# Spatial products of 32 sample tokens: operands of 128 partitions with zeros instead of 32 partitions

## The chip, the cores and the metric

The kernel runs on one core of a Trainium2 chip. The metric is the device time of one execution in microseconds (us); three runs of the kernel before gave a median of 2195.8. The core has TensorE (PE, whose weight loads the profile lists as PEld), VectorE (DVE), ScalarE (ACT), GpSimd (POOL) and SyncE (SP), and 16 DMA engines. In this kernel nearly all DMAs are issued from SP's queue, in order.

## What is computed

The reference is one inference step of a two-layer encoder for two groups of tokens that share the weights: 1024 prompt tokens and 32 sample tokens, of 1024 channels. Layer 0 mixes tokens with a spatial gate, layer 1 with pooling; each layer ends with a channel MLP of 4096. The change touches the spatial gate alone:

```python
def sgu_mixer(h, w_in, g_v, w_s, b_s, w_out, T):
    z = jax.nn.gelu(h @ w_in)
    u, v = jnp.split(z, 2, axis=-1)
    v = rmsnorm(v, g_v)
    vr = v.reshape(bsz, L // T, T, SGU_GROUPS, SGU_GROUP_DIM)
    w = w_s[:, :T, :T] * sgu_chunk_mask()[:T, :T].astype(w_s.dtype)
    s = jnp.einsum('gij,bnjgd->bnigd', w, vr)
    s = s + jnp.transpose(b_s[:, :T])[None, None, :, :, None]
    s = s.reshape(bsz, L, D_SGU)
    return (u * s) @ w_out, v
```

T is 128 for the prompt (8 chunks) and 32 for the sample (one chunk of 32 tokens). There are 8 groups of 256 channels. So each group has, besides the prompt's products that sum over 128 tokens, one product that sums over the 32 sample tokens.

## The kernel before

**Tiling.** Channels lie on the partitions and tokens on the columns. `TILES` (L27) cuts the tokens into three tiles: 384 and 384 prompt tokens, and 256 prompt tokens with the 32 sample tokens behind them (`npr` = 256, `nsm` = 32, `nch` = 2 chunks). Only the third tile has sample tokens. The large products are done in split precision: `products` (L910 to L917) issues three matmuls for each term, high by high (L915), high by low (L916) and low by high (L917). Helpers record all VectorE operations under L79.

**The gating stage.** The v half of the input product is computed first, with tokens on the partitions, and stored in DRAM as `vd`, one row for each token, the sample's 32 rows last. `mixes` (L357) then lists the passes over pairs of groups and tiles, and `sgu_item` (L1208) does two groups of one tile:

- `up` (L1241) computes the u half, matmuls into `pu` at L915 to L917, and an activation (L1251). Before its first product it calls `inputs`, and after it `factors`.
- `inputs` (L1217) takes a buffer `vl` of 128 partitions x 3 x 256 and loads the chunks of the group from `vd` (L1219), and in the third tile the 32 sample rows into partitions 0 to 31 of the last slice (L1224). `vl` comes from a ring of three buffers (`x3`), which other small tiles share.
- `factors` (L1228) multiplies the transposed and masked spatial weights `wt` by the reciprocal norms `rv` of the tokens: one 128x128 block for each chunk (L1235), and a 32x32 block for the sample (L1237).
- `gate` (L1254) does the spatial products for two halves k of the group: for each chunk one fp32 product over 128 partitions (L1263), and in the third tile one over 32 partitions and 32 columns (L1271), into the same PSUM bank `psp`. VectorE then applies gain and bias and multiplies by u.
- `down` (L1303) is the product with `w_out`, into `po`; it runs later, among the `up` of the next item.

Each fp32 product shows as two weight loads and two matmuls in the profile. A gate thus has 12 passes: 2 x 3 chunks x 2 in the first two tiles, and 2 x (2 chunks + 1 sample) x 2 in the third. There are 24 gates, 8 of them in the third tile.

**Order.** Outside the first stage, which is written out by hand, a scheduler orders the instructions on each engine, with the estimated times that `tick` and `weave` keep to place the weight stream among the products. Weights come by DMA into three `raw` buffers, ScalarE writes the high part (L423), VectorE the low part (L79), into a ring of 16 buffers that TensorE frees. GpSimd has work in the first microseconds (the identity, small loads) and two additions at the end (L1651).

Of the kernel before, what the change touches and what calls it, by code (L numbers as in the profile page):

```python
# [12 lines left out]
ALU = mybir.AluOpType  # L13
AX = mybir.AxisListType

P = 128
# [18 lines left out]
def tile_stream_encoder_step(  # L35
# [25 lines left out]
    nc = tc.nc  # L61
# [11 lines left out]
    def on_dve(op, fixed, rate):  # L73
        def run(out, *args, **kw):
            n = 1
            for k in out.shape[1:]:
                n *= k
            time["dve"] += fixed + n / rate
            return op(out, *args, **kw)  # L79

        return run
# [3 lines left out]
    ts = on_dve(nc.vector.tensor_scalar, 0.1, 930.0)  # L85
# [48 lines left out]
    def ps_up(name):  # L134
        return psum.tile([P, 512], F32, tag="pu", bufs=2, name=name)
# [7 lines left out]
    def t_m(name):  # L143
        return work.tile([P, 384], F32, tag="m", bufs=3, name=name)
# [7 lines left out]
    def t_x(name, shape):  # L152
        return work.tile(shape, F32, tag="x3", bufs=3, name=name)
# [756 lines left out]
    def products(ps, n, terms):  # L910

        last = len(terms) - 1
        tick(3 * len(terms) * (0.004 + n / 2265.0))
        for i, (wh, wl, rh, rl) in enumerate(terms):
            mm(ps[:, :n], wh, rh, start=i == 0, stop=False)  # L915
            mm(ps[:, :n], wh, rl, start=False, stop=False)  # L916
            mm(ps[:, :n], wl, rh, start=False, stop=i == last)  # L917
# [191 lines left out]
    rv = const.tile([P, 9], F32, name="rv")  # L1109
# [98 lines left out]
    def sgu_item(p, t, mix, after):  # L1208
        gs, tiles = mixes[p]
        last = t == tiles[-1]  # L1210
        n = ncol[t]
        col0, npr, nsm = TILES[t]
        nch = npr // P
        hid = []
        vls, wrs = {}, {}

        def inputs(g):  # L1217
            vl = vls[g] = t_x(f"vl{g}_{t}", [P, 3, 256])
            nc.sync.dma_start(  # L1219
                vl[:, :nch, :],  # L1220
                vd[col0 : col0 + npr, g * 256 : (g + 1) * 256].rearrange("(c p) d -> p c d", p=P),
            )
            if nsm:
                nc.sync.dma_start(  # L1224
                    vl[:nsm, nch, :], vd[SEQ : SEQ + nsm, g * 256 : (g + 1) * 256]
                )

        def factors(g):  # L1228
            wt, _, turn = mix[g]
            while turn:  # L1230
                turn.pop()()
            wr = wrs[g] = t_m(f"wr{g}_{t}")
            for c in range(nch):
                b = col0 // P + c
                ts(wr[:, c * P : (c + 1) * P], wt, rv[:, b : b + 1], None, op0=ALU.mult)  # L1235
            if nsm:
                ts(wr[:nsm, npr : npr + nsm], wt[:nsm, :nsm], rv[:nsm, 8:9], None, op0=ALU.mult)  # L1237

        us = []

        def up(g, k):  # L1241
            if k == 0:
                inputs(g)
            ps = ps_up(f"pu{g}_{t}_{k}")
            products(ps, n, up_terms(("u", p, g, k), t))
            if k == 0:
                factors(g)
            if last:
                w_finish(("u", p, g, k))
            u = t_m(f"u{g}_{t}_{k}")  # L1250
            act(out=u[:, :n], in_=ps[:, :n], func=AF.Gelu_apprx_tanh)  # L1251
            us.append(u)

        def gate(g):  # L1254

            vl, wr, bb = vls[g], wrs[g], mix[g][1]
            sps = []
            tick(0.48 * nch + 0.2)
            for k in range(2):
                sp = ps_dn(f"psp{g}_{t}_{k}")  # L1260
                sps.append(sp)
                for c in range(nch):
                    mm(  # L1263
                        sp[:, c * P : (c + 1) * P],
                        vl[:, c, k * P : (k + 1) * P],
                        wr[:, c * P : (c + 1) * P],
                        start=True,
                        stop=True,
                    )
                if nsm:  # L1270
                    mm(  # L1271
                        sp[:, npr : npr + nsm],
                        vl[:nsm, nch, k * P : (k + 1) * P],
                        wr[:nsm, npr : npr + nsm],
                        start=True,
                        stop=True,
                    )
            for k, sp in enumerate(sps):
                f = 2 * g + k
                s = t_c(f"s{g}_{t}_{k}")  # L1280
                stt(
                    out=s[:, :npr].rearrange("p (c j) -> p c j", j=P),
                    in0=sp[:, :npr].rearrange("p (c j) -> p c j", j=P),
                    scalar=gvT[:, f : f + 1],
                    in1=bb.unsqueeze(1).broadcast_to([P, nch, P]),
                    op0=ALU.mult,
                    op1=ALU.add,
                )
                if nsm:
                    stt(  # L1290
                        out=s[:, npr : npr + nsm],
                        in0=sp[:, npr : npr + nsm],
                        scalar=gvT[:, f : f + 1],
                        in1=bb[:, :nsm],
                        op0=ALU.mult,
                        op1=ALU.add,
                    )
                tt(out=s[:, :n], in0=s[:, :n], in1=us.pop(0)[:, :n], op=ALU.mult)
                a, b = t_hid("h", f"ush{g}_{t}_{k}"), t_hid("l", f"usl{g}_{t}_{k}")
                split(a, b, s, n)  # L1300
                hid.append((a, b))

        def down():  # L1303
            for d in range(KB):
                ps = ps_dn(f"po{gs[0]}_{t}_{d}")
                terms = []
                for j, (a, b) in enumerate(hid):
                    wh, wl = need_w(("o", p, gs[j // 2], d // 4))
                    o = (j % 2) * 512 + (d % 4) * P
                    terms.append((wh[:, o : o + P], wl[:, o : o + P], a[:, :n], b[:, :n]))  # L1310
                products(ps, n, terms)
                accumulate(t, d, ps, gs[0] == 0)
                if d == 0 and after is not None:
                    st = Stat(t, f"rs_{t}")
                if after is not None:
                    st.square(d)
                if last and d % 4 == 3:
                    for g in gs:
                        w_finish(("o", p, g, d // 4))
                weave(d % 2)  # L1320
            if after is not None:
                after(st)

        for j in range(4):
            up(gs[j // 2], j % 2)
            if j % 2 == 1:
                gate(gs[j // 2])
            weave()
            if j == 0:
                flush()  # L1330
        pending.append(down)
# [390 lines left out]
```

## Time and profile before

| | before |
|---|---|
| runs, median of 3 (lowest to highest) | 2195.8 us (2195.24 to 2196.72) |
| the profiled execution | 2196.44 us |
| its span, first to last instruction | 2194.7 us |
| mean granted TensorE clock | 0.998 |
| TensorE / VectorE / ScalarE / GpSimd busy | 99% / 63% / 45% / under 1% |
| the gating stage, first to last spatial product | 244.5 to 635.3 us |

How to read the lines of the profile. A timeline row gives start and duration in us, engine and line, operation, written<-read tiles by their names in the program, shapes and a count of merged instructions. For a matmul, "128*128 128x384" is the part of the array in use (partitions * columns of the stationary operand) and the moving operand. A row of a group gives the count, busy time and mean duration in ns, then the idle time of its engine just before and what ended it. A row of waits gives who waited for whom, the total in us, how many times and the longest. The ends of matmuls are modelled, so that two of them overlap in the record; starts are what to compare.

### The profile page before, as it was taken

The numbers are of one execution on the slowest core, as the hardware profiler recorded it, in microseconds if no ns is written. First come the engines' busy times: TensorE is split into PE (matmuls) and PEld (weight loads), VectorE is DVE, ScalarE is ACT, GpSimd is POOL, SyncE is SP. The second block draws the span as 40 slices with busy tenths as digits, with TensorE's granted clock in tenths as the row PEclk, the third lists the DMA queues.
The fourth block names the chain that finished last, engine by engine and source line by source line (L and its number), as shares of the span: only waits on it lengthen the run. The fifth ranks groups of instructions, "written<-read, shape, count | busy, mean of one in ns | idle before, by whom it ended". The sixth has DMA issues, their size and how long they took to land.

```text
span 2194.7 us, 33441 instructions
## 1 busy us (share of the span) xinstructions
PE 2177.2 (99%) x13383; PEld 2095.6 (95%) x13383; DVE 1374.9 (63%) x2431; ACT 987.9 (45%) x1683; POOL 5.4 (0%) x12
## 2 busy tenths in 40 slices
PE   8999999999999999999999999999999999999998
PEld 5777999999999999999999999999999999999998
DVE  6756656466769546575647779869675553523375
ACT  5533422234447552323445566666564542313355
POOL 0000000000000000000000000000000000000000
PEclk9999999999999999999999999999999999999999
DMA  8475633353437443344545466565454542302342
GB/s 292 163 240 166 193 97 121 91 156 104 138 101 233 130 150 120 106 133 123 179 128 163 139 189 186 161 196 156 143 171 135 162 154 60 106 10 77 99 123 108
DMA packets 354865, 312.99 MB, mean 143 GB/s; under 512 B 10834, under 2 KB 316538, under 8 KB 354708
## 3 DMA queue, kind: packets, MB, share of 16 engines
q1 hardware_dynamic: 354452, 310.61, 45.7%
q8 instruction: 105, 1.72, 0.3%
q14 instruction: 52, 0.43, 0.1%
q10 hardware_dynamic: 128, 0.14, 0.0%
q0 software_dynamic: 128, 0.09, 0.0%
HBM read 278.95 MB, written 31.84 MB: 142 GB/s over the span
## 4 chain that ended last, share of the span: by engine, by line
PE 98%; ACT 1%; DMA 0%; DVE 0%; issue 0%; POOL 0%; POOLq 0%; SPq 0%; ACTq 0%; DVEq 0%
PE pf L915 12%; PE pf L917 11%; PE pg L915 11%; PE pg L917 11%; PE pg L916 11%; PE pf L916 11%; PE pu L915 3%; PE pu L917 3%; PE po L915 3%; PE po L916 3%; PE po L917 3%; PE pu L916 3%; PE pv L942 2%; PE pv L943 2%; PE pv L944 2%; PE psp L1263 1%
## 5 line engine op out<-in xcount | busy, mean ns | idle before, releaser
L915 PE MATMUL pf<-hh,wh_up 128*128 128x384 f32 (+1 forms) x1536 | 502.6, 327 | 0.0
L915 PE MATMUL pg<-fh,wh_dn 128*128 128x384 f32 (+1 forms) x1536 | 498.0, 324 | 0.0
L917 PE MATMUL pf<-hh,wl_up 128*128 128x384 f32 (+1 forms) x1536 | 496.5, 323 | 0.0
L917 PE MATMUL pg<-fh,wl_dn 128*128 128x384 f32 (+1 forms) x1536 | 494.8, 322 | 0.0
L916 PE MATMUL pg<-fl,wh_dn 128*128 128x384 f32 (+1 forms) x1536 | 494.6, 322 | 0.0
L916 PE MATMUL pf<-hl,wh_up 128*128 128x384 f32 (+1 forms) x1536 | 490.5, 319 | 0.0
L915 PEld LDWEIGHTS pg<-fh,wh_dn 128*128 128x128 f32 x1536 | 288.8, 188 | 4.4 <-issue 3.3
L79 DVE TENSOR_TENSOR wl_up<-raw,wh_up 128x1024 fp32r<-128x1024 f32 x152 | 185.9, 1224 | 167.3 <-ACT wh_up L423 167.3
L915 PEld LDWEIGHTS pf<-hh,wh_up 128*128 128x128 f32 x1536 | 288.2, 188 | 1.3 <-issue 0.8
L916 PEld LDWEIGHTS pg<-fl,wh_dn 128*128 128x128 f32 x1536 | 288.6, 188 | 0.7
L916 PEld LDWEIGHTS pf<-hl,wh_up 128*128 128x128 f32 x1536 | 288.6, 188 | 0.4
L917 PEld LDWEIGHTS pg<-fh,wl_dn 128*128 128x128 f32 x1536 | 288.5, 188 | 0.0
L917 PEld LDWEIGHTS pf<-hh,wl_up 128*128 128x128 f32 x1536 | 288.0, 187 | 0.0
L423 ACT ACTIVATE wh_up<-raw 128x1024 fp32r<-128x1024 f32 x152 | 161.1, 1060 | 276.8 <-PE pf L916 214.3
L79 DVE TENSOR_TENSOR acc<-acc,pg 128x384 f32<-128x384 f32 (+1 forms) x336 | 174.0, 518 | 166.5 <-PE pg L917 165.3
L423 ACT ACTIVATE wh_dn<-raw 128x1024 fp32r<-128x1024 f32 x152 | 160.9, 1059 | 218.0 <-PE pg L916 180.9
L79 DVE TENSOR_TENSOR wl_dn<-raw,wh_dn 128x1024 fp32r<-128x1024 f32 x152 | 185.9, 1223 | 85.8 <-ACT wh_dn L423 85.6
L79 DVE SCALAR_TENSOR_TENSOR aa<-raw,csil,aa 128x512 f32<-128x512 f32 (+1 forms) x364 | 204.2, 622 | 2.0 <-DMA raw<-in_w_ada_dram 1.7
L1345 ACT ACTIVATE r<-pf 128x384 f32<-128x384 f32 (+1 forms) x192 | 86.5, 451 | 197.7 <-PE pf L917 197.5
L79 DVE TENSOR_TENSOR fl<-r,fh 128x384 fp32r<-128x384 f32 (+1 forms) x192 | 100.3, 522 | 104.3 <-ACT fh L1171 103.0
L915 PE MATMUL pu<-hh,wh_u 128*128 128x384 f32 (+1 forms) x384 | 127.9, 333 | 0.0
L915 PE MATMUL po<-ush,wh_o 128*128 128x384 f32 (+1 forms) x384 | 124.4, 324 | 0.0
(271 smaller groups left out, 2903.2 us busy)
## 6 DMA issues: line engine op xcount, KB each, us to landing
raw<-in_ffn_w_up_dram SPq DMA_DIRECT2D x152, 512.0 KB, 4.0
raw<-in_ffn_w_down_dram SPq DMA_DIRECT2D x152, 512.0 KB, 3.4
raw<-in_w_ada_dram SPq DMA_DIRECT2D x96, 512.0 KB, 4.1
raw<-in_sgu_w_in_dram SPq DMA_DIRECT2D x40, 512.0 KB, 4.4
xd<-acc SPq DMA_DIRECT2D x8, 1536.0 KB, 7.2
raw<-in_sgu_w_out_dram SPq DMA_DIRECT2D x24, 512.0 KB, 3.8
xo_r<-xd SPq DMA_DIRECT2D x32, 384.0 KB, 3.6
vd<-vt SPq DMA_DIRECT2D x32, 256.0 KB, 3.3
```

What stands on the lines that cost most here:

```text
L79: return op(out, *args, **kw)
L423: act(out=wh, in_=r, func=AF.Copy)
L915: mm(ps[:, :n], wh, rh, start=i == 0, stop=False)
L916: mm(ps[:, :n], wh, rl, start=False, stop=False)
L917: mm(ps[:, :n], wl, rh, start=False, stop=i == last)
L942: mm(ps[:m, :], a_h, wh[:, o : o + 512], start=k == 0, stop=False)
L943: mm(ps[:m, :], a_h, wl[:, o : o + 512], start=False, stop=False)
L944: mm(ps[:m, :], a_l, wh[:, o : o + 512], start=False, stop=k == KB - 1)
L1263: mm(sp[:, c * P : (c + 1) * P], vl[:, c, k * P : (k + 1) * P], wr[:, c * P : (c + 1) * P], start=True, stop=True,)
L1345: act(out=r[:, :n], in_=ps[:, :n], func=AF.Relu)
```

## The change

The rows of `vl` beyond the 32 sample rows are set to zero by GpSimd ahead of the small DMA, in the third tile only. The factor block of the sample becomes 128x32, with all 128 rows of `wt` and of `rv`, and both operands of the sample's product become 128 partitions high. The sum over partitions 32 to 127 adds zeros.

```diff
@@ inputs
             if nsm:
+
+                nc.gpsimd.memset(vl[:, nch, :], 0.0)
                 nc.sync.dma_start(
                     vl[:nsm, nch, :], vd[SEQ : SEQ + nsm, g * 256 : (g + 1) * 256]
                 )
@@ factors
             if nsm:
-                ts(wr[:nsm, npr : npr + nsm], wt[:nsm, :nsm], rv[:nsm, 8:9], None, op0=ALU.mult)
+                ts(wr[:, npr : npr + nsm], wt[:, :nsm], rv[:, 8:9], None, op0=ALU.mult)
@@ gate
                 if nsm:
                     mm(
                         sp[:, npr : npr + nsm],
-                        vl[:nsm, nch, k * P : (k + 1) * P],
-                        wr[:nsm, npr : npr + nsm],
+                        vl[:, nch, k * P : (k + 1) * P],
+                        wr[:, npr : npr + nsm],
                         start=True,
                         stop=True,
                     )
```

The built program has the same instructions in the same order on TensorE, VectorE, ScalarE and SP; GpSimd has eight more, the memsets of 128x256, in the order of the eight gates. Each small DMA into `vl` waits for its memset, and the first sample product of each gate waits for the memset too. The line numbers after the change are 2 higher from the small DMA on (L1226, L1239, L1265, L1273).

## The prediction

> **What bounds the kernel now.** I read the page first, for the engine that sets the end.
>
> ```profile
> PE 2177.2 (99%) x13383; PEld 2095.6 (95%) x13383; DVE 1374.9 (63%) x2431; ACT 987.9 (45%) x1683; POOL 5.4 (0%) x12
> ...
> PEclk9999999999999999999999999999999999999999
> ...
> PE 98%; ACT 1%; DMA 0%; DVE 0%; issue 0%; POOL 0%; POOLq 0%; SPq 0%; ACTq 0%; DVEq 0%
> ```
>
> TensorE is busy for 99% of the span, it makes up 98% of the chain that ended last, and its granted clock is 9 tenths or more in all 40 slices, so nothing is to be had from the clock. Next comes the view of waits, once for TensorE and once for all engines, to see whether time taken off TensorE would only turn into waiting.
>
> ```profile
> PE xT L590 <- DMA x_rows<-in_x_prompt_dram: 4.5, 1, 4.5
> PE pv L987 <- ACT hh L888: 2.0, 2, 1.1
> ...
> PE yT L1668 <- ACT yo L1669: 0.3, 2, 0.2
> PE pn_r_2x L804 <- ACT xt L1425: 0.2, 1, 0.2
> ...
> ACT wh_up L423 <- PE pf L916: 214.3, 94, 18.3
> ```
>
> TensorE's waits are short and mostly at the start: the first x rows (4.5 us) and the first pv products (2.0). The later rows, yT and pn_r_2x, come to 0.5 us. In the other direction ScalarE waits 214.3 us for TensorE before it splits weights: the weight pipeline is held back by TensorE, not the reverse. A microsecond taken off TensorE in the gating stage should therefore reach the end.
>
> "Busy" hides one thing, since the ends of matmuls are modelled: how far apart they start. So I read the timeline of TensorE around a gate of the third token tile, the only tile that holds the sample tokens, and around a gate of the first tile. Columns: start, duration, line, out<-in, shapes, count.
>
> ```profile
> 316.74 0.60 PE L1263 MATMUL psp<-wr,vl 128*128 128x128 f32 x4
> 317.27 0.40 PE L1271 MATMUL psp<-wr,vl 32*128 32x32 f32 x2
> 317.60 0.71 PE L1263 MATMUL psp<-wr,vl 128*128 128x128 f32 x4
> 318.25 0.40 PE L1271 MATMUL psp<-wr,vl 32*128 32x32 f32 x2
> 318.58 0.40 PE L915 MATMUL pu<-hh,wh_u 128*128 128x288 f32 x1
> 318.82 0.29 PE L916 MATMUL pu<-hl,wh_u 128*128 128x288 f32 x1
> 318.95 0.29 PE L917 MATMUL pu<-hh,wl_u 128*128 128x288 f32 x1
> ```
>
> ```profile
> 244.63 1.50 PE L1263 MATMUL psp<-wr,vl 128*128 128x128 f32 x12
> 245.88 0.42 PE L915 MATMUL pu<-hh,wh_u 128*128 128x384 f32 x1
> 246.14 0.33 PE L916 MATMUL pu<-hl,wh_u 128*128 128x384 f32 x1
> 246.31 0.33 PE L917 MATMUL pu<-hh,wl_u 128*128 128x384 f32 x1
> ```
>
> Both gates issue 12 matmul passes (each fp32 product shows as two). In the first tile they follow each other closely. In the third tile the four passes before L1271 take 317.27 - 316.74 = 0.53 us to the next start, and each pair of L1271 takes 0.33 us, though it streams only 32 columns. The weight loads say why:
>
> ```profile
> 316.61 0.54 PEld L1263 LDWEIGHTS psp<-wr,vl 128*128 128x128 f32 x4
> 317.27 0.29 PEld L1271 LDWEIGHTS psp<-wr,vl 32*128 32x128 f32 x2
> 317.60 0.52 PEld L1263 LDWEIGHTS psp<-wr,vl 128*128 128x128 f32 x4
> ...
> 2185.03 0.75 PEld L1623 LDWEIGHTS pn_last<-ones,sq_rf 128*128 128x128 f32 x6
> ...
> L915 PEld LDWEIGHTS pg<-fh,wh_dn 128*128 128x128 f32 x1536 | 288.8, 188 | 4.4 <-issue 3.3
> ```
>
> Among loads over 128 partitions the next one starts while a matmul still runs: the load group of 316.61 begins 0.13 us before its first matmul. At L1271 the first load starts together with its own matmul (317.27 both), and after it the load of 317.60 starts with the matmul of 317.60. At each change between 32 and 128 partitions, both ways, the next load waits as if the array had to be emptied first. The row of pn_last shows that the partitions do it and not the few columns: its matmuls stream 2 columns over 128 partitions, and its loads still follow at (0.75 - 0.19) / 5 = 0.11 us, with 0.19 the mean of one load (188 ns, the page's L915 row).
>
> **The change part by part.**
>
> *The matmuls at L1271* (4 passes in each gate of the third tile, eight gates, 32 passes) take operands of 128 partitions instead of 32. That removes four changes of partition count per gate. The new form, 32 columns over 128 partitions, is in no row. The nearest rows bound its step from both sides in columns: 0.11 us for 2 columns in pn_last, and for 128 columns the 12 passes of the first tile's gate, which take 246.14 - 244.63 = 1.51 us with the 384-column matmul behind them and 1.34 without its 0.17 (246.31 - 246.14): 1.34 / 12, again 0.11. I take 0.11.
>
> So a gate of the third tile should run like one of the first tile. I measure each from the first pass to the start of the second matmul behind the gate. Where the matmul behind has 384 columns I expect the 1.51 us above; where it has 288, which steps by 0.13 (318.82 to 318.95) instead of 0.17, I expect 1.47. Now the gate at 316.74 takes 318.82 - 316.74 = 2.08, which gives 0.61 us. The other kind is followed by 384 columns:
>
> ```profile
> 325.07 0.61 PE L1263 MATMUL psp<-wr,vl 128*128 128x128 f32 x4
> 325.61 0.40 PE L1271 MATMUL psp<-wr,vl 32*128 32x32 f32 x2
> 325.95 0.71 PE L1263 MATMUL psp<-wr,vl 128*128 128x128 f32 x4
> ...
> 326.92 0.44 PE L915 MATMUL pu<-hh,wh_u 128*128 128x384 f32 x1
> 327.20 0.33 PE L916 MATMUL pu<-hl,wh_u 128*128 128x384 f32 x1
> ...
> L1271 PE MATMUL psp<-wr,vl x32: 271/282/292, 317.3 to 635.3; 32*128 32x32 f32 x32
> L1271 PEldq EVENT_SEMAPHORE  x4: 51/51/51, 323.2 to 631.8; - x4
> ```
>
> It takes 327.20 - 325.07 = 2.13 us, so 0.62 us goes. The x32 row (minimum, median, maximum in ns) shows passes that hardly differ from 317.3 to 635.3 us. Sum: 4 x 0.61 + 4 x 0.62 = 4.9 us less.
>
> *One more wait ahead of each first sample product*: it now also waits for the memset, besides its DMA. The x4 row above is such an extra wait, an instruction of 0.05 us on TensorE's queue: four of the eight gates have one today. The first stands at 323.2, over 2 us before its load, and that gate's pair still takes 0.34 us (325.61 to 325.95) against 0.33. Behind the waiting load stands all that TensorE has left, so a late memset would stop it; but the queue's run-ahead covers the instruction itself: I take nothing, and uncovered 8 x 0.05 = 0.4 us.
>
> *The memset, new ahead of L1224,* puts eight instructions of 128x256 on GpSimd, which does nothing between the first microseconds and the end. No row shows this size; these are the nearest:
>
> ```profile
> masks.py:197 POOL MEMSET ident<- 128x128 f32 x1 | 0.2, 204 | 0.3 <-POOLq L1703 0.3
> L1651 POOL TENSOR_TENSOR xlast<-zlast,xlast 32x512 f32<-32x512 f32 x2 | 2.5, 1263 | 2184.7 <-ACT zlast L1650 2184.7
> ...
> 550.16 0.37 SPq L1219 DMA_DIRECT2D vl<-vd  x1
> 550.58 0.46 SPq L1224 DMA_DIRECT2D vl<-vd  x1
> 553.89 0.53 SPq L852 DMA_DIRECT2D xd<-acc  x1
> ...
> 567.63 0.49 PE L1263 MATMUL psp<-wr,vl 128*128 128x128 f32 x3
> ...
> DMA to landing us min/median/max: 2.4/2.8/4.6
> ```
>
> Twice 0.20 is 0.41 us; the slowest GpSimd row is 1.26. I take 0.41, the like operation. It waits for the same free buffer as the DMA of L1219 does, in the same order, and not for that DMA's landing. The small DMA at L1224 then waits for the memset and follows L1219 by 0.42 us today, so it is held for about nothing, or by 1.26 - 0.42 = 0.84 us at the upper bound. Behind it on SP's queue stand weight and residual loads, here the store of xd 3.3 us later. What covers this is the distance to use: in the tightest of the eight cases the DMA issued at 550.58 lands by about 553.4 (median landing 2.8) and its gate starts at 567.63, 14 us later. Without that cover it would cost at most 8 x 0.84 = 6.7 us. Should VectorE be slowed while GpSimd writes, that is at most 8 x 0.41 = 3.3 us of VectorE, which has 37% of the span to spare.
>
> *The factors at L1237* grow from 32x32 to 128x32 on VectorE; no row has 128x32.
>
> ```profile
> L79 DVE TENSOR_SCALAR wr<-wt,rv 128x128 f32<-128x128 f32 x64 | 15.0, 281 | 0.3
> L79 DVE TENSOR_SCALAR wr<-wt,rv 32x32 f32<-32x32 f32 x8 | 1.8, 223 | 0.0
> ```
>
> The bounds are 0.22 and 0.28 us, at most 8 x 0.06 = 0.5 us on an engine busy for 63%; I take 0.22, as the columns are the same, and nothing for the end, since TensorE waits for almost nothing (above).
>
> No other instruction moves: the order on TensorE, VectorE, ScalarE and SP stays, only GpSimd gets eight.
>
> **Sum.** The profiled execution lasted 2196.4 us (span 2194.7 and 1.7 around it), so it would take 2191.5. The median of the runs, 2195.8, lies 0.6 below the profiled one; by the same sum it becomes 2190.9.
>
> **The rivals.**
>
> *The loads over 128 partitions cannot run ahead of the small matmuls.* Then the four sample passes of a gate step by a whole load, 0.19 us, instead of 0.11: 4 x 8 x 0.08 = 2.6 us is given back, and the time is 2193.5. Against it: pn_last loads at 0.11 us ahead of matmuls of 2 columns. [...]
>
> *The gain does not arrive, or the gaps stay*: the emptying belongs to the small product itself and not to its partitions, or a later wait takes the gain. Then 2195.8. For it: the new form is in no row. Against it: pn_last and the 214.3 us for which ScalarE waits for TensorE.
>
> *Slower: GpSimd holds SP's queue.* If the memset comes late by D, the DMA behind it goes out late by D, and from D = 14 us the gate at 567.63 waits for it by D - 14. The gain is gone at D = 19. With D = 28 the time is 2190.9 + 14 = 2204.9. For it: no row shows GpSimd at work in the middle of this kernel. Against it: no row of GpSimd is longer than 1.26 us.
>
> **How the numbers follow.** About 0.2% (4.4 us, here 2191.4) is what a measurement of this kernel can tell from no change. Forecast: 0.87; loads not ahead: 0.04; no gain: 0.05; slower: 0.04. The forecast's 4.9 us is close to 4.4; runs before lay 0.6 below to 0.9 above their median, so I count one in nine of the forecast's cases as within 0.2%. Faster: 0.87 x 0.89 = 0.77. Same: 0.10 + 0.04 + 0.05 = 0.19. Slower: 0.04. Range: the forecast with the runs' scatter and 0.4 us of uncovered waits is 2190.3 to 2192.2; I widen it to 2190.0 to 2192.5, which leaves out the three rivals.
>
> **What would show it.** Right: in the timeline of a third-tile gate the sample passes read 128*128 128x32, their loads start about 0.11 us apart and ahead of the matmul, and first pass to second matmul behind the gate takes 1.47 or 1.51 us instead of 2.08 or 2.13; GpSimd shows eight memsets near 0.41 us; TensorE's waits gain no row on vl or the memset. Wrong: steps of 0.2 us at the sample passes, a wait of TensorE for GpSimd, or a shortened gating stage (316 to 636 us) with a later stage longer by as much.

## The result and the profile after

| | before | after |
|---|---|---|
| median of 21 runs (lowest to highest) | 2195.43 us (2194.79 to 2198.31) | 2192.03 us (2190.61 to 2194.11) |
| the profiled execution | 2196.44 us | 2190.76 us |
| its span | 2194.7 us | 2188.9 us |

The ratio is 0.9981, 95% interval 0.9974 to 0.9987. The change made the kernel faster, by 0.19% at this median. When the changed kernel was run again (below) the ratio was 0.998, 0.9971 to 0.9989, and all 32 of its runs together have a median of 2191.12 us against 2195.47 for the 54 runs of before beside them. The prediction was 2190.9, and it set 2191.4 as the line from which a gain can be told from no change: the first median falls short of that line, though its interval leaves out 1, and the median of all 32 runs is past it. Why the two medians of one kernel differ by over a microsecond is told below, where the two groups of runs are.

The first two lines are from the page of the changed kernel; busy time and share for each engine, then the chain that ended last.

```profile
PE 2171.4 (99%) x13383; PEld 2093.1 (96%) x13383; DVE 1375.2 (63%) x2431; ACT 988.1 (45%) x1683; POOL 7.9 (0%) x20
...
PE 98%; ACT 0%; DVE 0%; DMA 0%; issue 0%; POOL 0%; POOLq 0%; ACTq 0%; DVEq 0%
```

Same bound, same number of matmuls (13383); TensorE's busy time is 5.8 us less, VectorE's and ScalarE's the same. GpSimd has 20 instructions in place of 12.

The timeline of TensorE around the first gate of the third tile, in the changed kernel:

```profile
315.65 0.60 PE L1265 MATMUL psp<-wr,vl 128*128 128x128 f32 x4
316.09 0.31 PE L1273 MATMUL psp<-wr,vl 128*128 128x32 f32 x2
316.24 0.69 PE L1265 MATMUL psp<-wr,vl 128*128 128x128 f32 x4
316.76 0.31 PE L1273 MATMUL psp<-wr,vl 128*128 128x32 f32 x2
...
317.12 0.29 PE L916 MATMUL pu<-hl,wh_u 128*128 128x288 f32 x1
```

and the weight loads of the same stretch:

```profile
315.52 0.54 PEld L1265 LDWEIGHTS psp<-wr,vl 128*128 128x128 f32 x4
315.98 0.30 PEld L1273 LDWEIGHTS psp<-wr,vl 128*128 128x128 f32 x2
316.21 0.53 PEld L1265 LDWEIGHTS psp<-wr,vl 128*128 128x128 f32 x4
316.65 0.30 PEld L1273 LDWEIGHTS psp<-wr,vl 128*128 128x128 f32 x2
```

The gate takes 317.12 - 315.65 = 1.47 us from its first pass to the second matmul behind it; before it was 2.08. The pair of L1273 takes 316.24 - 316.09 = 0.15 us to the next start in place of 0.33, and its loads now begin 0.11 us ahead of it (315.98) in place of together with it. The loads follow one another evenly through the whole gate: four from 315.52 to 315.98, two to 316.21 and four to 316.65, 0.11 to 0.12 us each. A gate with 384 columns behind it, again from the timeline of TensorE in the changed kernel:

```profile
323.38 0.61 PE L1265 MATMUL psp<-wr,vl 128*128 128x128 f32 x4
...
324.89 0.34 PE L916 MATMUL pu<-hl,wh_u 128*128 128x384 f32 x1
```

324.89 - 323.38 = 1.51 us, before 2.13. All eight gates are alike: 1.47 us where 288 columns stand behind, 1.51 or 1.52 where 384 do. These rows are from the view of line 1273 of the changed kernel (count, then minimum, median and maximum in ns, first and last start):

```profile
L1273 PEld LDWEIGHTS psp<-wr,vl x32: 192/192/192, 316.0 to 629.2; 128*128 128x128 f32 x32
L1273 PE MATMUL psp<-wr,vl x32: 195/236/276, 316.1 to 629.2; 128*128 128x32 f32 x32
L1273 PEldq EVENT_SEMAPHORE  x8: 51/51/51, 313.8 to 626.3; - x8
```

The second matmul behind the last gate starts at 629.61, before at 635.81: TensorE is 6.2 us ahead when the gating stage ends. Of that, the eight gates are 4.9 us; the lead goes from 1.1 us to 1.7 over the first of them, to 2.3 over the second, and so on in steps of 0.6. Where is the rest from? TensorE was ahead already at the first gate of the stage. From the timelines of TensorE in the changed kernel:

```profile
243.54 1.50 PE L1265 MATMUL psp<-wr,vl 128*128 128x128 f32 x12
...
355.60 0.34 PE L917 MATMUL pu<-hh,wl_u 128*128 128x384 f32 x1
355.77 1.50 PE L1265 MATMUL psp<-wr,vl 128*128 128x128 f32 x12
357.03 0.42 PE L915 MATMUL pu<-hh,wh_u 128*128 128x384 f32 x1
```

and in the kernel before:

```profile
357.90 0.34 PE L917 MATMUL pu<-hh,wl_u 128*128 128x384 f32 x1
358.19 1.60 PE L1263 MATMUL psp<-wr,vl 128*128 128x128 f32 x12
359.55 0.42 PE L915 MATMUL pu<-hh,wh_u 128*128 128x384 f32 x1
```

The first gate starts at 243.54, before at 244.63: 1.1 us, where the two programs are the same on TensorE. A later gate of the first tile lost (358.19 - 357.90) - (355.77 - 355.60) = 0.12 us at its start and 1.36 - 1.26 = 0.10 within it, 0.2 together, which is gone here; when the changed kernel was run again, this gate lost time again (1.62 us in place of 1.51), so the 0.2 does not belong to the change. So 1.1 + 0.2 + 4.9 = 6.2, and by the spans only 2194.7 - 2188.9 = 5.8 arrives: 0.4 us is given back behind the gating stage, 0.3 of it at the very end. The start of the last three transposes, from the timelines of TensorE, is at 2186.68 before and here in the changed kernel at

```profile
2180.58 0.53 PE L1407 MATMUL yT<-ident,acc 128*128 128x128 f32 x3
```

so from there to the end of the span it takes 2194.7 - 2186.68 = 8.0 us before and 2188.9 - 2180.58 = 8.3 us after. The DMA view of the last outputs says what is late. In the changed kernel, from 2184 to 2188 us (queue, packets, MB, share of 16 engines; then issues with KB and median us to landing):

```profile
q14 instruction: 1, 0.01, 0.5%
...
out_dram<-xlast SPq DMA_DIRECT2D x2, 256.0 KB, 3.2
```

and before, from 2190 to 2194 us, the same moment of its own end:

```profile
q1 hardware_dynamic: 457, 0.81, 55.6%
q10 hardware_dynamic: 96, 0.13, 13.7%
...
out_dram<-xlast SPq DMA_DIRECT2D x2, 256.0 KB, 2.6
```

The last store from SyncE lands after 3.2 us in place of 2.6, and in its midst stands one packet of the queue that the profile calls q14, instruction. In the kernel before, that queue's last packet comes at 2194.07 us, behind the stores. Half of the later landing is hidden: before, ScalarE's last store (issued at 2191.1, landed after 2.3 us) landed 0.3 us behind SyncE's (2190.5 and 2.6), and now SyncE's is the last. Where that packet comes from is a question of its own below.

GpSimd's memset, from the view of its line in the changed kernel:

```profile
L1225 POOL MEMSET vl<- x8: 306/311/315, 266.7 to 587.7; 128x256 f32 x8
```

It takes 0.31 us. TensorE's view of waits has the rows of before and none on `vl` or on GpSimd.

### The profile page after: what moved, and what is told of

Its sections match the earlier page's. It is cut to its first block, busy times and chain, and to the rows that moved or that the text cites. A ratio compares the mean times of both kernels' runs of the same rounds, so it can differ in the third digit from the quotient of the medians.

```text
span 2188.9 us, 33479 instructions
## 1 busy us (share of the span) xinstructions
PE 2171.4 (99%) x13383; PEld 2093.1 (96%) x13383; DVE 1375.2 (63%) x2431; ACT 988.1 (45%) x1683; POOL 7.9 (0%) x20
## 4 chain that ended last, share of the span: by engine, by line
PE 98%; ACT 0%; DVE 0%; DMA 0%; issue 0%; POOL 0%; POOLq 0%; ACTq 0%; DVEq 0%
PE pf L915 12%; PE pf L917 11%; PE pg L915 11%; PE pg L917 11%; PE pg L916 11%; PE pf L916 11%; PE pu L915 3%; PE pu L917 3%; PE po L915 3%; PE po L916 3%; PE po L917 3%; PE pu L916 3%; PE pv L942 2%; PE pv L943 2%; PE pv L944 2%; PE psp L1265 1%
```

## The experiments

Three questions were open: whether it is the change of partition count that costs the 4.9 us; why the medians moved by less than that; and what moved the end by 0.3 us. Theory for the first: the gaps come with each switch between an operand of 32 partitions and one of 128, four times a gate (a gate took 2.08 us before and takes 1.47 now). Rivals: the small product itself is slow, whatever surrounds it; or the gain comes from something else in the change (the memset, or the waits that come with it).

| run | median, us (lowest to highest) | ratio to before, 95% interval |
|---|---|---|
| after again | 2190.86 (2190.47 to 2194.14) | 0.998, 0.9971 to 0.9989 |
| memset alone | 2195.89 (2195.42 to 2199.07) | 1.0001, 0.9992 to 1.001 |
| 64 partitions | 2195.89 (2195.36 to 2198.16) | 1.0002, 0.9993 to 1.0011 |
| 96 partitions | 2191.77 (2190.33 to 2194.64) | 0.998, 0.9972 to 0.9989 |
| sample products grouped | 2193.28 (2192.94 to 2194.76) | 0.999, 0.9981 to 0.9999 |
| busy start | 2192.70 (2191.33 to 2194.97) | 0.9984, 0.9976 to 0.9993 |
| zero rows in DRAM | 2193.45 (2191.76 to 2196.06) | 0.9988, 0.9979 to 0.9997 |
| 29 more GpSimd instructions | 2195.73 (2195.06 to 2197.05) | 1.0001, 0.9992 to 1.001 |
| 5 more SyncE transfers | 2195.83 (2195.36 to 2197.45) | 1.0, 0.9991 to 1.0009 |
| after, 24 more SyncE transfers | 2204.16 (2203.46 to 2206.89) | 1.0039, 1.0026 to 1.0051 |
| after, 20 of them late | 2191.21 (2190.67 to 2193.40) | 0.9979, 0.997 to 0.9988 |
| after, 10 of them at the end | 2190.78 (2190.00 to 2192.42) | 0.9977, 0.9968 to 0.9986 |

### The changed kernel again, and the memset alone

The changed kernel ran unchanged, as a measure for the others.

> The changed kernel as it is. Theory (the four changes between 32 and 128 partitions in each third-tile gate are what is saved, 0.305 us for each sample product): the eight gates take 1.47 or 1.51 us from first pass to second matmul behind, and a profile whose matmuls run at full clock around 18 to 22 us has TensorE 4.9 us ahead of the kernel before at the last gate, plus or minus what the start gives. Rival (the start or another stage gave the gain): the gates keep 1.47 but the time goes back to within 1 us of before.

The second is the kernel before with only this:

```diff
             if nsm:
+                nc.gpsimd.memset(vl[:, nch, :], 0.0)
                 nc.sync.dma_start(
```

> Only the memset is added; the sample products stay on 32 partitions. Theory: the memset is covered, so gates stay at 2.08 and 2.13 us and the time within 0.5 us of before, 2195 to 2196. Rival (the new wait or GpSimd's writes cost something that the 128-partition products hide): 0.5 to 3 us slower than before, with a wait of TensorE or a longer gate. Second rival (the memset itself moves the start or the DMAs to better places): 1 us or more faster.

The repeat was faster again, and it allows a comparison like with like: in its profile the first gate starts at 244.66 us, before at 244.63, and the second matmul behind the last gate at 630.89, before at 635.81. So 4.9 us come from the gating stage alone, with nothing gained ahead of it; the spans differ by 2194.7 - 2190.2 = 4.5 us. The memset alone changes nothing in the gates, which took 2.08 and 2.13 us as before, and nothing in the time that can be measured. So the gain is in the operands of the matmul and the factors, not in the memset and its waits. Its last output, though, landed after 3.1 us, as in the changed kernel.

### 64 and 96 partitions

The changed kernel, with the memset, the factors and the product over 64 partitions, and another over 96:

```diff
-                nc.gpsimd.memset(vl[:, nch, :], 0.0)
+                nc.gpsimd.memset(vl[:64, nch, :], 0.0)
...
-                ts(wr[:, npr : npr + nsm], wt[:, :nsm], rv[:, 8:9], None, op0=ALU.mult)
+                ts(wr[:64, npr : npr + nsm], wt[:64, :nsm], rv[:64, 8:9], None, op0=ALU.mult)
...
-                        vl[:, nch, k * P : (k + 1) * P],
-                        wr[:, npr : npr + nsm],
+                        vl[:64, nch, k * P : (k + 1) * P],
+                        wr[:64, npr : npr + nsm],
```

> The sample products on 64 partitions, 32 of them zero. Theory (every change of the used part of the array to or from 128 partitions costs): the gaps stay, gates 2.08 and 2.13 us, time as before, 2195 to 2196. Rival (only products on 32 partitions are slow): gates 1.47 and 1.51, time as after the change, 2190.6 to 2192.4.

> The sample products on 96 partitions. [...] Rival (any count of partitions other than that of the neighbours costs): gates 2.08 and 2.13, time as before, 2195 to 2196.

With 64 partitions the whole cost is back. The timeline of TensorE at the first gate of the third tile of that version:

```profile
315.90 0.60 PE L1265 MATMUL psp<-wr,vl 128*128 128x128 f32 x4
316.44 0.41 PE L1273 MATMUL psp<-wr,vl 64*128 64x32 f32 x2
...
317.99 0.29 PE L916 MATMUL pu<-hl,wh_u 128*128 128x288 f32 x1
```

317.99 - 315.90 = 2.09 us, as at 32 partitions. With 96 partitions the same timeline reads

```profile
317.08 0.60 PE L1265 MATMUL psp<-wr,vl 128*128 128x128 f32 x4
317.52 0.31 PE L1273 MATMUL psp<-wr,vl 96*128 96x32 f32 x2
...
318.55 0.29 PE L916 MATMUL pu<-hl,wh_u 128*128 128x288 f32 x1
```

318.55 - 317.08 = 1.47 us, as with 128. So zeros up to 128 are not needed, and it isn't the number of partitions as such that costs: 32 and 64 cost the same, 96 and 128 nothing. The weight loads part the two in the same way: with 64 the first load of the pair starts together with its matmul (316.44 us both), as with 32, and with 96 it starts 0.11 us ahead (317.41 against 317.52), as with 128. Why 96 goes with 128 and 64 with 32 is not shown.

### Two switches for each gate in place of four

The kernel before, with the two sample products behind both halves' chunk products rather than each behind its own:

```diff
-                if nsm:
+            if nsm:
+                for k, sp in enumerate(sps):
                     mm(
```

> The kernel before, with the two sample products of a gate, on 32 partitions as they were, issued one behind the other after all chunk products: two changes of partition count in a gate instead of four, no memset, the same products. Theory (the cost lies in the changes): half of the gain, 0.305 us a gate, so gates of 1.78 and 1.82 us and 2.4 us off the time, 2193.1. Rival (the cost lies in the 32-partition product itself, 0.33 us a pair wherever it stands): gates stay at 2.08 and 2.13, time 2195.5.

This keeps 32 partitions and all the passes, and halves the switches. The timeline of TensorE at a gate with 384 columns behind it:

```profile
323.56 1.05 PE L1263 MATMUL psp<-wr,vl 128*128 128x128 f32 x8
324.54 0.63 PE L1272 MATMUL psp<-wr,vl 32*128 32x32 f32 x4
...
325.38 0.34 PE L916 MATMUL pu<-hl,wh_u 128*128 128x384 f32 x1
```

325.38 - 323.56 = 1.82 us, midway between 2.13 and 1.51. Half of the switches, half of the gain: the gap belongs to the switch and not to the small product. The rival that puts the gap down to the product falls here. One excursion to 32 partitions and back thus costs (2.13 - 1.51) / 2 = 0.31 us. The weight loads of this gate show where it goes:

```profile
323.43 0.99 PEld L1263 LDWEIGHTS psp<-wr,vl 128*128 128x128 f32 x8
324.54 0.52 PEld L1272 LDWEIGHTS psp<-wr,vl 32*128 32x128 f32 x4
325.10 0.19 PEld L915 LDWEIGHTS pu<-hh,wh_u 128*128 128x128 f32 x1
```

With 0.19 us for one load, the last of the eight starts at 324.23, 0.31 us ahead of the next one, and the last of the four at 324.87, 0.23 us ahead of the next. Within both groups the step is 0.11 us, so loads over 32 partitions follow each other as closely as loads over 128: only the two switches are longer, by 0.20 us there and 0.12 back. The time followed too: eight of the eleven runs lie around 2193.08 us, 2.3 less than the 2195.38 of the lower group of before beside them, where 2.4 was expected.

### Why the median moved by 3.4 us: two groups of runs

The runs of nearly every kernel here lie in two groups 1.3 to 1.5 us apart. Of the 32 runs of the changed kernel 17 lie around 2190.76 and 13 around 2192.27; of the 54 of before 35 lie around 2195.39 and 18 around 2196.73 (the rest higher still). From lower group to lower group the change is worth 2195.39 - 2190.76 = 4.6 us. In the first measurement 11 of 21 runs of the changed kernel fell in the upper group and 6 of 21 of before, so the median moved by 3.4.

What tells the groups apart shows in the windows of the profile around 20 us (busy time and count of each engine, then the granted TensorE clock, DMA share, GB/s). The kernel before, whose profiled execution of 2196.44 us is of the upper group:

```profile
17.80:18.20 0.40, 0.40 (x3) 0.32 (x3) 0.40 (x2) 0.40 (x1) 0.00 (x0) 1.00 0.99 358
18.30:21.60 3.30, 3.30 (x9) 2.57 (x8) 1.39 (x3) 2.86 (x7) 0.00 (x0) 0.50 1.10 349
21.75:22.25 0.50, 0.50 (x4) 0.40 (x3) 0.43 (x3) 0.00 (x0) 0.00 (x0) 1.00 1.11 348
```

The changed kernel, profiled at 2190.76 us, of the lower:

```profile
18.30:21.60 3.30, 3.30 (x16) 2.65 (x15) 1.65 (x3) 3.16 (x6) 0.00 (x0) 1.00 1.10 349
```

One stretch of 3.3 to 3.55 us at half the clock: 0.50 granted from 18.30 to 21.60 us in the kernel before, 1.00 up to 18.20 and from 21.75 on, and 9 matmuls in place of 16. That is the 1.1 us by which TensorE was behind at the first gate: in the profiles with this stretch the first gate starts between 244.6 and 245.5 us, in the unchanged ones without it between 243.4 and 244.0. What sets its length and its place is not shown. Eleven profiles here have this start unchanged and nothing else that adds a microsecond (before, after, after again, memset alone, 64, 96, grouped, 29 on GpSimd, 5 on SyncE, and the last two). In the six with the stretch the profiled time is of the upper group, in the five without it of the lower. The mean clock of the whole run, 0.998 with it and 0.999 without, hardly shows it.

I tried to move a run from one group to the other. TensorE waits for data between 10 and 17 us (0.94, 0.56 and 1.11 us in the kernel before, ahead of its matmuls at 11.59, 15.09 and 16.64); into these waits went eight products of the identity with itself, whose results nobody reads:

```diff
+    def busy(n):
+        for _ in range(n):
+            mm(early_ps[4][:, :P], ident, ident, start=True, stop=True)
...
         turn_vectors()
+        busy(2)
...
+        busy(2)
         fold()
+        busy(4)
         stream_to("w", ("v", 0, 0))
```

> The changed kernel with eight more products of the identity (results overwritten later) where TensorE waits between 10 and 17 us. The profiles so far differ in one stretch of 3.4 us from about 18.4 us on, in which the granted clock is one half in some executions and full in others, and the runs of one kernel fall into two groups 1.4 us apart. Theory (the half clock is what sets the groups, and comes from too little work before it): the half-clock stretch is gone from the profile and nearly all runs lie in the lower group, near 2190.7. Rival (the stretch comes regardless of the work before it, or the groups have another cause): the runs still fall into two groups, 2190.7 and 2192.2, or the added products lengthen the start and all are later by up to 1 us.

The profile of this version, which is that of its fastest run, shows no stretch at half clock, but its first gate starts at 244.36 us, 0.8 us later than in the changed kernel: the products lengthened the start. The runs do not gather in a lower group: they spread from 2191.33 to 2194.97, with a median 1.9 us above the lower group of the changed kernel. So the stretch goes with the upper group, and whether its absence can be had by such products is not shown. It is left as an association.

### The zeros from DRAM, without GpSimd

The changed kernel with 96 zero rows stored behind the sample rows of `vd` in the first stage (VectorE sets the buffer to zero), so that one DMA of three chunks brings them and neither the memset nor the small DMA is needed:

```diff
-    vd = dram.tile([SEQ + DEC, SGU], F32, name="vd")
+    vd = dram.tile([SEQ + P, SGU], F32, name="vd")
...
         if b == 8:
+            nc.vector.memset(vt, 0.0)
...
-                vl[:, :nch, :],
-                vd[col0 : col0 + npr, g * 256 : (g + 1) * 256].rearrange("(c p) d -> p c d", p=P),
+                vl[:, : nch + (nsm > 0), :],
+                vd[col0 : col0 + npr + (P if nsm else 0), g * 256 : (g + 1) * 256].rearrange("(c p) d -> p c d", p=P),
...
-                nc.gpsimd.memset(vl[:, nch, :], 0.0)
```

> The sample products stay on 128 partitions, but the zeros come from DRAM: the v stage stores 128 rows for the sample, 96 of them zero (four memsets of 128x512 on VectorE), and one DMA loads the three chunks of a third-tile group; no memset on GpSimd, no second DMA, no wait for GpSimd. Theory (the gates give 4.9 us, and the changed kernel loses 0.3 us of it at the end, where the last output DMA from SP lands 3.2 us after its issue instead of 2.6, because of the instructions added on GpSimd): gates of 1.47 and 1.51, last landing back at 2.6, lower group of runs 0.3 us below the changed kernel, near 2190.4. Rival (the later landing comes with the shorter gates or with chance): landing stays at 3.1 to 3.2 and the time is that of the changed kernel. Second rival (VectorE's memsets hold the v stage): TensorE loses up to 2 us before the gating stage.

The gates took 1.47 us and the last output landed after 2.6 us again, as the theory of the added GpSimd and SyncE instructions has it. Yet the version is slower than the changed kernel by over 2 us. In the profiled execution the loss lies ahead of the third tile's gates, at a gate of the first tile. Its view of waits of TensorE has a row that neither the kernel before nor the changed one has (96 partitions has it with 0.2 us, the 24 transfers with 1.0), and the timeline shows what follows:

```profile
PE psp L1260 <- DVE wr L79: 1.8, 1, 1.8
```

```profile
255.60 2.38 PE L1260 MATMUL psp<-wr,vl 128*128 128x128 f32 x12 [1.83 <-DVE wr L79]
...
258.10 0.52 PE L916 MATMUL pu<-hl,wh_u 128*128 128x384 f32 x1
258.42 0.52 PE L917 MATMUL pu<-hh,wl_u 128*128 128x384 f32 x1
```

TensorE waited 1.83 us for the factors, and the matmuls behind then step by 0.32 us (258.10 to 258.42), where 384 columns step by 0.17: the window from 254.5 to 259.5 us has a granted clock of 0.67. One short wait cost the wait and then a stretch of slower matmuls: at the next gate TensorE is 3.9 us later than in the changed kernel (283.67 against 279.78). VectorE was itself behind by then: it had sat idle for 1.68 us before the operation at 249.05 us (`vst`), whose first loads SyncE issued at 238.78 and 244.83 us, in the changed kernel at 235.53 and 240.17. That these loads held it is likely, but the profile names no releaser, and why SyncE issued them later stays open.

### What moves the last output

An instruction packet falls amid the last stores in the changed kernel and with the memset alone, and not before, nor in the grouped version (landing 2.6). The memsets add instructions on GpSimd, and on SyncE five waits: the view of the small DMA's line has five semaphore instructions in the changed kernel and none before. The first try lengthened GpSimd's program alone, in the kernel before:

```diff
+    for _ in range(29):
+        nc.gpsimd.memset(junk1, 0.0)
     sgu_stack.close()
```

> The kernel before with 29 memsets of 128x1 on GpSimd in the gating stage, as many instructions as the eight memsets and their 21 waits, which nothing waits for. Theory (the number of instructions on GpSimd moves a code load into the last output DMAs): the last output DMA from SP lands 3.1 to 3.2 us after its issue instead of 2.6, and the lower group of runs is 0.3 to 0.4 us above before, 2195.6 to 2195.7, with gates as before. Rival (it takes the memsets' waits or data): landing 2.6, time as before, lower group 2195.3.

The last output landed after 2.6 us. GpSimd's length is not it. The second lengthened SyncE's, with transfers of 16 elements that nobody reads, again in the kernel before:

```diff
+    for i in range(5):
+        with tc.issue_after(list(loads.values())[-1]):
+            nc.sync.dma_start(spare[:, 16 * i : 16 * i + 16], c_sample[0:1, 16 * i : 16 * i + 16])
     sgu_stack.close()
```

> Before, with five transfers of 16 elements each added on SyncE's queue behind the gating stage, whose results nobody reads. Theory (SyncE's longer program in the changed kernel moves a load of program code into the last output transfers): the last output lands after 3.1 to 3.2 us where before has 2.6, a code packet is shown beside it, and the lower group of run times is 0.3 to 0.4 us above before's 2195.3. Rival (something else in the change moves it): the last landing stays 2.6 us and the times are before's within 0.1 us. Both: gates unchanged at 2.08 and 2.13 us.

Here the packet is back. The DMA view of that version from 2189 to 2190 us:

```profile
q14 instruction: 1, 0.01, 2.7%
...
out_dram<-xlast SPq DMA_DIRECT2D x2, 256.0 KB, 3.2
```

The last store landed after 3.2 us, and from the last transposes to the end it took 8.3 us, as after. The five transfers on SyncE are the only change, and they moved the packet from behind the last stores into them; so it is taken to be a load of SyncE's program, though whose instructions it carries is not shown. Over all fourteen profiles the two go together: in the seven with this packet among the last stores the last landing takes 3.1 to 3.3 us and the end comes 8.2 to 8.3 us after the last transposes, in the other seven 2.5 to 2.6 and 7.7 to 8.0. That the packet itself delays the store is not shown. In the times it is a hint at most. The ratio is 1.0. The lower group of this version lies at 2195.58 against 2195.21 for the runs of before beside it; the memset alone (2195.69) and 64 partitions (2195.81), which have the late landing too, lie 0.3 and 0.4 us above theirs (2195.39). But with 29 instructions on GpSimd and no late landing it is 0.3 below (2195.25 against 2195.53), so a difference of 0.3 is within what the groups scatter.

The last three versions tried to have it back in the changed kernel, by making SyncE's program longer still, so that the packet comes earlier. First 24 transfers, at the same place:

```diff
+    for i in range(24):
+        with tc.issue_after(list(loads.values())[-1]):
+            nc.sync.dma_start(spare[:, 16 * i : 16 * i + 16], c_sample[0:1, 16 * i : 16 * i + 16])
```

> After, with 24 such small transfers added on SyncE's queue. Theory (the place of the code load follows the length of SyncE's program): the load comes well ahead of the last output, which lands after 2.6 us again, and the lower group of run times is about 0.3 us below after's 2190.75, near 2190.4. Rival (the place doesn't follow SyncE's length): the last landing stays 3.1 to 3.2 us and the times are after's. Both: gates 1.47 and 1.52 us.

This was slower by 13 us than the changed kernel, neither of the two expectations. SyncE's timeline and TensorE's waits:

```profile
640.33 13.78 SPq L1445 DMA_DIRECT2D spare<-in_c_sample_dram  x16
```

```profile
PE pf L916 <- ACT r L1348: 10.0, 1, 10.0
```

Sixteen small transfers in a row occupy SyncE for 13.78 us, 0.9 us each, and the weight loads behind them on the queue are late (the next stands at 654.20 us); TensorE waits 10.0 us, until 667.10 us, and its matmuls then step by 0.32 us again (667.58 to 667.90), where 384 columns step by 0.17. The last output landed after 2.6 us, with no instruction packet beside it, as the theory has it. The next two put the transfers where less stands behind them: 20 behind the last weight load, then 10 between the last store of y and the stores of the last block.

```diff
         def last():
 
+            for i in range(20):
+                with tc.issue_after(list(loads.values())[-1]):
+                    nc.sync.dma_start(spare[:, 16 * i : 16 * i + 16], c_sample[0:1, 16 * i : 16 * i + 16])
```

> After, with 20 small transfers of 16 elements added on SyncE's queue behind the last weight load, where only the last block of x and three stores of y are queued behind them. Theory (the place of the code load follows the length of SyncE's program, and its falling into the last output costs 0.3 us): no code packet beside the last output, the last output lands after 2.6 us, and the lower group of run times is about 0.3 us below after's 2190.75, near 2190.4. Rival (the place of the code load does not matter for the time, or does not follow the length): the last landing stays 3.1 to 3.2 us or the lower group stays at 2190.75. If the transfers hold up the last block of x, TensorE shows a wait of some us behind 2142 us, and the time says nothing.

```diff
             dsts = [dst for _, _, dst in blocks]
+            for i in range(10):
+                with tc.issue_after(ystore[-1]):
+                    nc.sync.dma_start(spare[:, 16 * i : 16 * i + 16], c_sample[0:1, 16 * i : 16 * i + 16])
...
-                nc.sync.dma_start(dst, yo[:w, :])
+                ystore.append(nc.sync.dma_start(dst, yo[:w, :]).ins)
```

> After, with 10 small transfers of 16 elements on SyncE's queue between the last store of y and the stores of the last block, where SyncE has some 16 us to spare and nothing else is queued behind them. Theory (the place of the code load follows the length of SyncE's program; in the run with 20 transfers it had left the last output, but the stores of y held up TensorE by 0.4 us): no code packet beside the last output, from the last matmul's start to the end 7.5 to 7.7 us in place of 8.1, TensorE as in after, the lower group of run times 0.3 to 0.5 us below after's 2190.75: 2190.2 to 2190.45. Rival (the gain was the other side of the held-up stores): 8.1 us and 2190.75 as in after.

With 20, the last store landed after 2.5 us and the end came 2188.8 - 2181.01 = 7.8 us after the last transposes, in place of 8.3; but these started 0.43 us later (2180.58 in the changed kernel). In its timeline:

```profile
2152.92 16.44 SPq L1621 DMA_DIRECT2D spare<-in_c_sample_dram  x14
2169.45 1.83 SPq L1676 DMA_DIRECT2D out_dram<-yo  x3
...
2181.01 0.53 PE L1408 MATMUL yT<-ident,acc 128*128 128x128 f32 x3
```

The stores of y stand at 2163.41 in the changed kernel, so they were held up by 6 us. But it is not this that made TensorE late, as the expectation of the next version has it: this execution was 0.28 us late at its first gate (243.82 against 243.54), 0.30 at its last (628.40 against 628.10) and 0.39 in SyncE's load at 2120.77 us, all ahead of the first of these transfers at 2148.51. And in the times nothing was gained: nine of the eleven runs lie around 2191.18, where 2190.4 was expected. With 10 at the end the stores of y go out as before. The packet of q14 has left the stores, and the last output lands after 2.6 us; the DMA view of that version from 2182 to 2190 us has one other instruction packet, of queue q8; its row, and the last transposes:

```profile
q8 instruction: 1, 0.02, 1.1%
```

```profile
2182.57 0.53 PE L1408 MATMUL yT<-ident,acc 128*128 128x128 f32 x3
```

The end comes 2190.6 - 2182.57 = 8.0 us after them, the 8.0 of before (the packet of q8 stands at the last matmuls, ahead of the stores, as one does before). So in the traces the 0.3 us is had back. In the times it is not shown: seven of ten runs lie from 2190.00 to 2190.85, with a median of 2190.70 against 2190.76 for the lower group of the changed kernel, where 2190.2 to 2190.45 was expected. The median over all runs, 2190.78, is the lowest of all versions, but within the intervals it is the changed kernel's.

## Why the prediction was right

*The bound.* Time taken off TensorE in the gating stage reached the end: TensorE's busy share and its waits stayed, and no row of its waits grew by more than 0.1 us in its place. Right, but for the last output, which is no matter of TensorE (below).

*The gates.* Predicted 1.47 and 1.51 us, measured 1.47 and 1.51, at all eight; 4 x 0.61 + 4 x 0.62 = 4.9 us went. The reason given, that the next load waits at each change between 32 and 128 partitions, is what the grouped version shows (half the changes, half the gain: 1.82 us between 2.13 and 1.51); that the array is emptied meanwhile is a reading that no trace shows. The 64- and 96-partition versions narrow the reason: it is not any change of the number, since 64 costs what 32 does (2.09 us) and 96 is free (1.47). The step of 0.11 us is that of the weight loads, which keep it through the gate (315.52 to 316.65). The starts of the matmuls do not: a sample pair takes 0.15 us rather than 2 x 0.11, and the four chunk passes behind it 316.76 - 316.24 = 0.52 us rather than 0.44. The two differences cancel, as they must if the loads set the pace.

*The extra wait on TensorE.* The waits at L1273 went from 4 to 8, the first 2.2 us ahead of its load, and the gates have their predicted length: nothing, as taken.

*The memset.* 0.31 us rather than 0.41: twice the 128x128 row was too much. It is off the path, and so is the small DMA: TensorE waits for neither. The memset alone left the time as it was.

*The factors.* One over 128x32 takes 0.24 us, between the bounds of 0.22 and 0.28. VectorE's busy time went from 1374.9 to 1375.2 us, and TensorE does not wait for them more than before. Right.

*"No other instruction moves: the order on TensorE, VectorE, ScalarE and SP stays."* The order does stay, but SyncE gets five waits, and this is the step that missed something: with them a packet of q14, instruction, falls among the last stores, and 0.3 us of the gain was given back in the profiled execution. That the small DMA waits for the memset stood in the text; that the wait is an instruction on SyncE, whose only effect seen is on where that packet falls, didn't; the section on the change, which has the same instructions on SP, leaves these five out as well.

*The sum.* From lower group to lower group 4.6 us, against 4.9 less the 0.3 of the last output: they agree. The median of the first measurement moved by less, 3.4, since more of its runs fell in the upper group (11 of 21, against 6 of 21 of before). The prediction's 0.6 us between profiled execution and median is the same matter: the profiled execution before was of the upper group. That the forecast of 2190.9 lies so near the lower group's 2190.76 is partly luck: it starts from 2195.8, 0.4 above the lower group of before, and takes off 4.9 where 4.6 came, and these two nearly cancel. And that the first median of 2192.03 lies in the range is owed to its width; the two groups, which moved that median, are not in the prediction.

*The rivals.* Loads over 128 partitions that can't run ahead of the small matmuls: refuted by the load at 315.98, 0.11 us ahead of its matmul. No gain: refuted. GpSimd holding SyncE's queue: 0.31 us each, no wait of TensorE; that a queue held for long does stop TensorE is seen with the 24 transfers, sixteen of which held it for 13.78 us; TensorE waited 10.0 us behind them.

## What to carry to other kernels

A small fp32 product over 32 or 64 partitions amid products over 128 paid 0.31 us here for the way there and back, which the busy share counts as work; compare starts, and look whether a weight load begins with its own matmul rather than ahead of it. Zeros beyond the data, up to 96 partitions, took the price away (a gate of 1.47 us in place of 2.08), since the memsets that wrote them, 0.31 us each with 128, came off the path; putting the small products side by side, without padding, halved it (1.82 us, between 2.13 and 1.51). Where a gain of a few microseconds is to be judged, look first whether the runs fall in groups, and compare within a group.

## What the runs showed of the hardware that was not expected

- 64 partitions cost as much as 32 (2.09 us a gate), and 96 as little as 128 (1.47). In the grouped version the way to 32 partitions cost 0.20 us and the way back 0.12; loads over 32 partitions in a row step by 0.11 us there.
- A stretch of 3.3 to 3.55 us at half clock (0.50 granted from 18.30 to 21.60 us in the kernel before, 1.00 in the changed one) is there in some executions of a kernel and not in others, and goes with 1.4 us of the time.
- With the zero rows in DRAM, a wait of 1.83 us of TensorE was followed by matmuls in steps of 0.32 us instead of 0.17, at a mean granted clock of 0.67 from 254.5 to 259.5 us; with the 24 transfers, one of 10.0 us was followed by steps of 0.32 us too.
- Five instructions more on SyncE, 1.5 ms ahead of the end, moved a packet of q14, instruction, from behind the last stores into them, and the last store then landed after 3.2 us in place of 2.6.
- Transfers of 16 elements from DRAM to DRAM in a row held SyncE's queue for 0.6 to 1.2 us each: 3.73 us for six, 9.26 for ten, 13.78 for sixteen, 16.44 for fourteen.
